# Rows spread over partitions by DMA through DRAM instead of by TensorE, halves swapped by VectorE, biases made three products at a time

## The chip, the cores and the metric

One NeuronCore of a Trainium2 chip runs the whole program in one launch. The metric is device time in microseconds, the median of several runs. Instructions run on TensorE (PE; its weight loads are shown apart, as PEld), VectorE (DVE), ScalarE (ACT) and GpSimd (POOL). DMAs are issued from the queues of SP, ACT and POOL.

## The reference, cut to what matters

Two blocks run on 512 tokens of width 1024, all in float32. The first has two hybrid layers; each holds sparse attention with an index (DSA), stick-breaking attention, and an mLSTM, whose outputs are gated and merged. The second has a feed-forward part, a mixing layer (an S5 state-space scan, dilated attention in three patterns, cross attention to a memory) and another feed-forward part. The change touches four places:

```python
# mLSTM: a weight exp(b_t - b_s + i_s - m_t) for every pair (t, s); m_t is a row over tokens, one per head
w_intra = jnp.exp(log_d - m_row[..., None])
# dilated attention: scores get a bias from rel_table by the bucket of the distance, per pattern and head;
# the three patterns' outputs are summed with shares that are a softmax over the patterns, per token and head
# S5: complex numbers with real and imaginary parts on 64 partitions each; a rotation needs both parts
x_re, x_im = abar_re * x_re - abar_im * x_im, abar_re * x_im + abar_im * x_re
```

## The kernel before, in words

Activations stand feature by feature: 128 features on partitions, 512 tokens along the free axis. Every big product is split in three (`three`, L292 to L294), with high and low parts of both factors in F32R: a weight block comes by DMA on SP's queue as `raw` (L255), ACT casts it to `whi` (L260) and DVE forms `wlo` (L261). A 512-column F32R product is one pass of PE. A product of plain F32, as in the four places below, is two passes with two weight loads (PE rows count passes).

The program is written as one stream of instructions. Its framework (Tile) orders each engine's instructions at build time from the dependencies and from tile slots in rings (`row`, `fr`, PSUM banks `b0` to `b7`), with the order of the text as priority; weight loads are raised by an offset (`woff`). On the chip each engine then keeps that order. So PE's stream mixes stages: a product with few columns stands between products of another stage, and topk rounds on DVE (`dsa_choose`, L606 and L607, needed by `dsa` at the end of a layer) stand wherever DVE had room. In the mixing layer `together` (L1182) interleaves three streams by costs: `mix_products`, `ssm` and `attention`; the last ends with `shares`, whose result `oa` is needed by the first `wup` product (L1157 on).

The four places, in order of time:

- **mLSTM rows** (`ml_gates` L756, `mlstm` L824). A scan on DVE (L814) leaves `M`, 4 partitions (heads) by 512 tokens. For each head a product of a one-hot column of the identity with `M` (L860) puts that head's row on all 128 partitions, in the PSUM bank of `av`; ACT reads it in the exponentials of L866. 2 layers x 4 heads = 8 products.
- **Biases** (`biases` L1365, called between the two halves of the first layer's mLSTM). Per pattern DVE copies the bias table out to 128 columns per head (L1374, L1375); per head one product with one-hot buckets (L1379, 33 rows) gives 128 equal rows, ACT copies them (L1381), a POOL DMA stores them in `bd` (L1382). 12 products. `dilated_qkv` reads `bd` in the mixing layer (L1390).
- **SSM halves** (`ssm` L1719). Rotation into and out of the scan needs the other half's product: `y = sin * p` over 128 partitions (L1751, L1764), a product with a permutation that swaps the halves (L1755, L1766), an add or subtract from PSUM (L1756, L1768). 4 groups x 2 = 8 products.
- **Shares** (`shares` L1475). Per pattern: 4 transposes bring the shares to 4 partitions (L1496, shown under the helper's L490), ACT copies them (L1498), two products with 4 rows spread them over 64 partitions per head (L1501), and DVE multiplies the stored outputs `od` by them (L1505, L1509), reading PSUM. 12 transposes, 6 products.

The constants of the permutation, the spreading and a selection matrix `sel` are part of one tile loaded at the start (L1832); `sel` is copied once to F32R (L1833).

Of the kernel before, what the change touches and what calls it, by code (L numbers as in the profile page):

```python
# [8 lines left out]
F32 = mybir.dt.float32  # L9
# [8 lines left out]
P = 128  # L18
S = 512
D = 1024  # L20
NB = 4
# [66 lines left out]
def constants():  # L88
    parts = []
    at = 0  # L90

    def put(name, a):
        nonlocal at
        a = np.asarray(a, np.float32).reshape(P, -1)
        CONST[name] = (at, a.shape[1])
        at += a.shape[1]
        parts.append(a)

    i = np.arange(P)
# [5 lines left out]
    sel = np.zeros((P, P))  # L105
    for r in range(P):
        if r % 64 < 16:
            sel[r, r % 64] = 1.0
            sel[r, 64 + r % 64] = 1.0
    put("sel", sel)  # L110
# [9 lines left out]
    sp = np.zeros((P, 2, P))  # L120
    for h in range(4):
        sp[h, h // 2, 64 * (h % 2):64 * (h % 2) + 64] = 1.0
    put("spread", sp)
    put("swap", np.roll(np.eye(P), 64, axis=1))
    put("oz", np.tile([1.0, 0.0], (P, 4)))
    return np.concatenate(parts, axis=1)

# [58 lines left out]
def prepare(x):  # L186
    x = {k: np.asarray(v) for k, v in x.items()}
    out = {}
    out["consts"] = constants()
    out["vecs"] = vectors(x)  # L190
    out["xT"] = np.ascontiguousarray(x["x"][0].T.reshape(8, P, S).transpose(1, 0, 2))
    w = x["w_in"]
# [32 lines left out]
class Prog:  # L225
# [530 lines left out]
    def ml_gates(self, l):  # L756
# [58 lines left out]
        self.mlM = M  # L815
# [8 lines left out]
    def mlstm(self, l, W, u):  # L824
# [32 lines left out]
        for e in range(2):  # L857
            h = 2 * u + e
            pm = self.av()
            nc.tensor.matmul(pm, self.c("ident")[0:4, h:h + 1].to_broadcast([4, P]), self.mlM, start=True, stop=True)  # L860
# [504 lines left out]
    def biases(self):  # L1365

        nc, ap = self.nc, self.ap
        rel = self.t(ap, [32, 12], tag="rel")
        nc.gpsimd.dma_start(rel, self.A["rel"])
        oh = self.t(ap, [P, 896], tag="r4", bufs=2)[0:33]  # L1370
        nc.gpsimd.dma_start(oh, self.A["oneh"])
        for p in range(3):
            relb = self.row().rearrange("p (h n) -> p h n", h=4)
            nc.vector.memset(relb[32:33], 1.0)  # L1374
            nc.vector.tensor_copy(relb[0:32], rel[:, 4 * p:4 * p + 4].unsqueeze(2).to_broadcast([32, 4, P]))  # L1375
            w, at, n = self.BANDS[p]
            for h in range(4):
                ps = self.lt()
                nc.tensor.matmul(ps[:, :w], relb[0:33, h, :], oh[:, at:at + w], start=True, stop=True)  # L1379
                r = self.row()  # L1380
                nc.scalar.copy(r[:, :w], ps[:, :w])  # L1381
                nc.gpsimd.dma_start(self.bd[4 * p + h][0:P * w].rearrange("(p w) -> p w", w=w), r[:, :w])  # L1382
# [92 lines left out]
    def shares(self):  # L1475
# [14 lines left out]
        nc.vector.reciprocal(sm, sm)  # L1490
        acc = []
        for p in range(3):
            nc.vector.tensor_mul(sh[:, p, :, 0], sh[:, p, :, 0], sm)
            ps = self.lt()
            for b in range(NB):
                self.tr(ps[0:4, b * P:(b + 1) * P], sh[:, p, b, 0, :])  # L1496
            wt = self.row()
            nc.scalar.copy(wt[0:4, :], ps[0:4, :])  # L1498
            for m in range(2):
                ps = self.lt()  # L1500
                nc.tensor.matmul(ps, self.c("spread")[0:4, m * P:(m + 1) * P], wt[0:4, :], start=True, stop=True)  # L1501
                o = self.fr()
                nc.sync.dma_start(o, self.od[:, 2 * p + m, :])
                if p == 0:
                    nc.vector.tensor_mul(o, o, ps)  # L1505
                    acc.append(o)
                else:
                    t = self.row()
                    nc.vector.tensor_mul(t.rearrange("p (i r) -> p r i", r=4), o.rearrange("p (r i) -> p r i", r=4),  # L1509
                                         ps.rearrange("p (i r) -> p r i", r=4))  # L1510
# [207 lines left out]

    def ssm(self, W, sp):  # L1719
# [11 lines left out]
        for mt in range(4):  # L1731
# [19 lines left out]
            nc.vector.tensor_mul(y, sin, p)  # L1751
            nc.vector.tensor_mul(x, cos, p)
            yield True
            p = self.bank("py")
            nc.tensor.matmul(p, self.c("swap"), y, start=True, stop=True)  # L1755
            nc.vector.tensor_add(x, x, p)  # L1756
# [7 lines left out]
            nc.vector.tensor_mul(y, sin, w)  # L1764
            p = self.bank("py")
            nc.tensor.matmul(p, self.c("swap"), y, start=True, stop=True)  # L1766
            nc.vector.tensor_mul(x, cos, w)
            nc.vector.tensor_sub(x, x, p)  # L1768
# [23 lines left out]
    def run(self):  # L1792
# [14 lines left out]
        self.gd = dp.tile([16, 32, 240], F32, name="gd")  # L1807
        self.kd = dp.tile([P, 4, 256], F32, name="kd")
# [5 lines left out]
        with tc.tile_pool(name="at", bufs=1, reuse_waits="tile") as ap:  # L1814
# [18 lines left out]
            nc.scalar.copy(self.selr, self.c("sel"))  # L1833
# [45 lines left out]
```

## Time and profile before

| | us |
|---|---|
| median of 3 runs | 2619.22 (2613.62 to 2619.58) |
| profiled execution | 2615.3 |
| its span, first to last instruction | 2613.5 |
| PE busy in the span | 2568.2 |
| PE weight loads busy | 2113.5 |
| DVE busy | 1673.0 |
| ACT busy | 1179.3 |
| POOL busy | 265.9 |

A row of the timeline has the start of an instruction in microseconds from the start of the span, its length, engine, line, operation, output and inputs, shape and how many are joined in the row (x2); in brackets the idle time of the engine before it and what ended that. Lengths of products overlap, so what one costs PE is read from the starts of its neighbours.

### The profile page before, as it was taken

Reading aid. Unit: us, or ns where it says so; the run is one execution under the profiler, and the core shown is the slowest. Engines: PE = TensorE matmul, PEld = TensorE weight load, DVE = VectorE, ACT = ScalarE, POOL = GpSimd, SP = SyncE. Lnnn points to the kernel's source line nnn. Section 1 sums busy time; section 2 is a strip of 40 time slices with the busy share of each in tenths; the row PEclk is TensorE's granted clock in tenths of the full one; section 3 lists DMA queues with packets and bytes.
Section 4 is the critical chain, followed back from the end, with each engine's and each line's share of the span. In section 5 each row is a group of like instructions: output and inputs, shape, how many; then the busy total and the mean of one; then the engine's idle time right before and its main releaser. Section 6 shows DMA issues by size and latency. Waiting matters only on the chain.

```text
span 2613.5 us, 36025 instructions
## 1 busy us (share of the span) xinstructions
PE 2568.2 (98%) x13206; PEld 2113.5 (81%) x13206; DVE 1673.0 (64%) x3696; ACT 1179.3 (45%) x2290; POOL 265.9 (10%) x573
## 2 busy tenths in 40 slices
PE   8999999999999999999999999999999999999998
PEld 8888778788888777878888888877876778888798
DVE  8999975654699998665479665374333445555423
ACT  6665656743466565663342332233444233333322
POOL 0010000110000000001002782000000100000000
PEclk9999999999999999999999999999999999999999
DMA  6222232353322223235333334354433444322332
GB/s 191 85 101 85 93 107 97 104 178 125 113 73 90 85 89 114 88 113 178 121 130 106 133 124 150 106 170 144 119 93 115 158 153 151 107 97 97 121 89 81
DMA packets 115105, 305.56 MB, mean 117 GB/s; under 512 B 29210, under 2 KB 36506, under 8 KB 114928
## 3 DMA queue, kind: packets, MB, share of 16 engines
q1 hardware_dynamic: 87760, 236.23, 27.7%
q0 software_dynamic: 18576, 60.17, 6.6%
q10 hardware_dynamic: 8592, 6.87, 0.8%
q8 instruction: 104, 1.70, 0.3%
q14 instruction: 73, 0.60, 0.1%
HBM read 259.41 MB, written 43.79 MB: 116 GB/s over the span
## 4 chain that ended last, share of the span: by engine, by line
PE 75%; DVE 8%; ACT 3%; issue 1%; DMA 1%; SPq 0%; ACTq 0%; DVEq 0%; POOLq 0%
PE b L292 22%; PE b L293 22%; PE b L294 22%; PE b L490 3%; DVE wlo L261 1%; PE b L633 1%; DVE row L745 1%; PE b L684 1%; PE b L1447 1%; DVE row L744 1%; DVE row L747 1%; DVE row L743 1%; DMA row<-xd 0%; DVE keep L607 0%; PE b L1466 0%
## 5 line engine op out<-in xcount | busy, mean ns | idle before, releaser
L261 DVE TENSOR_TENSOR wlo<-raw,whi 128x1024 fp32r<-128x1024 f32 (+1 forms) x398 | 481.4, 1210 | 505.7 <-ACT whi L260 503.6
L260 ACT CAST whi<-raw 128x1024 fp32r<-128x1024 f32 (+1 forms) x398 | 412.9, 1037 | 646.8 <-PE b L293 486.1
L292 PE MATMUL b<-h,whi 128*128 128x512 f32 x1632 | 642.6, 394 | 0.0
L293 PE MATMUL b<-h,whi 128*128 128x512 f32 x1632 | 642.6, 394 | 0.0
L294 PE MATMUL b<-h,wlo 128*128 128x512 f32 x1632 | 641.0, 393 | 0.4 <-DVE wlo L261 0.4
L292 PEld LDWEIGHTS b<-h,whi 128*128 128x128 f32 x1632 | 307.8, 189 | 62.1 <-issue 2.3
L294 PEld LDWEIGHTS b<-h,wlo 128*128 128x128 f32 x1632 | 307.6, 188 | 61.5 <-DVE wlo L261 0.8
L293 PEld LDWEIGHTS b<-h,whi 128*128 128x128 f32 x1632 | 307.6, 188 | 59.6 <-issue 1.3
L292 PE MATMUL b<-hn,whi 128*128 128x512 f32 x320 | 129.9, 406 | 0.3 <-ACT hn L247 0.3
L294 PE MATMUL b<-hn,wlo 128*128 128x512 f32 x320 | 129.0, 403 | 0.0
L293 PE MATMUL b<-hn,whi 128*128 128x512 f32 x320 | 128.4, 401 | 0.1
L293 PE MATMUL b<-wlo,h 128*128 128x256 f32 x384 | 109.5, 285 | 0.0
L294 PE MATMUL b<-whi,h 128*128 128x256 f32 x384 | 109.2, 284 | 0.0
L292 PE MATMUL b<-whi,h 128*128 128x256 f32 x384 | 109.2, 284 | 0.0
L490 PE MATMUL b<-cst,row 128*128 128x128 f32 x452 | 88.9, 288 | 18.8 <-DVE row L747 11.0
L490 PEld LDWEIGHTS b<-cst,row 128*128 128x128 f32 x452 | 53.3, 143 | 63.1 <-issue 17.8
L1025 ACT ACTIVATE row<-row 128x512 f32<-128x512 f32 x44 | 27.8, 632 | 123.2 <-DVE row L1024 99.4
L292 PE MATMUL b<-whi,g 128*128 128x256 f32 x288 | 82.1, 285 | 0.0
L294 PE MATMUL b<-whi,g 128*128 128x256 f32 x288 | 82.1, 285 | 0.0
L293 PE MATMUL b<-wlo,g 128*128 128x256 f32 x288 | 81.9, 284 | 0.0
L292 PE MATMUL b<-yb,whi 128*128 128x512 f32 x192 | 75.9, 396 | 0.0
L294 PE MATMUL b<-yb,wlo 128*128 128x512 f32 x192 | 75.5, 393 | 0.0
(591 smaller groups left out, 5240.7 us busy)
## 6 DMA issues: line engine op xcount, KB each, us to landing
raw<-in_win_dram SPq DMA_DIRECT2D x190, 512.0 KB, 3.7
raw<-in_ffn_in_dram SPq DMA_DIRECT2D x88, 512.0 KB, 3.7
raw<-in_ffn_down_dram SPq DMA_DIRECT2D x40, 512.0 KB, 3.5
raw<-in_wbr_dram SPq DMA_DIRECT2D x24, 512.0 KB, 3.4
mxd<-fr POOLq DMA_DIRECT2D x48, 256.0 KB, 2.6
fr<-mxd POOLq DMA_DIRECT2D x48, 256.0 KB, 3.9
raw<-in_wout_dram SPq DMA_DIRECT2D x24, 512.0 KB, 3.7
yd<-row POOLq DMA_DIRECT2D x24, 256.0 KB, 2.6
```

What stands on the lines that cost most here:

```text
L260: nc.scalar.copy(hi, raw)
L261: nc.vector.tensor_sub(lo, raw, hi.bitcast(F32))
L292: mm(ps, a[0], b[0], start=first, stop=False)
L293: mm(ps, a[0], b[1], start=False, stop=False)
L294: mm(ps, a[1], b[0], start=False, stop=last)
L490: self.nc.tensor.transpose(out, in_, self.c("ident"))
L633: self.nc.tensor.matmul(o[:, c], V(sb), PT[i][:, sb, c], start=sb == 0 and i == 0, stop=sb == 3 and i == 1)
L684: nc.tensor.matmul(p[:, :nn], Q[h][:, tb * P:(tb + 1) * P], kk[i][:, :nn], start=i == 0, stop=i == 1)
L743: nc.vector.scalar_tensor_tensor(e[:, :n], e[:, :n], 1.0, st[:, :n], op0=ALU.min, op1=ALU.mult)
L744: nc.vector.scalar_tensor_tensor(sg[:, :n], sg[:, :n], 0.0, e[:, :n], op0=ALU.max, op1=ALU.add)
L745: nc.vector.tensor_tensor_scan(e[:, :n][:, ::-1], st[:, :n][:, ::-1], self.one.to_broadcast([P, n]), 1.0, op0=ALU.mult, op1=ALU.min)
L1025: nc.scalar.activation(th, t, AF.Tanh, scale=0.5)
```

## The change

- mLSTM: `M` is stored to a DRAM tile `md` after the scan, and each head's row is loaded from it with a broadcast over 128 partitions into an SBUF tile `pm`, both on POOL's queue. The tile shares a slot with `R` for odd heads.
- Biases: one product per pattern with the table's 4 columns as weights gives 4 rows; ACT copies them, POOL stores them in `br`, and four POOL DMAs per pattern copy a row, broadcast, from `br` to `bd`.
- Shares: all 12 columns are transposed together, 4 transposes in all; one copy, one store to `wd`, and 12 loads (64 partitions each), all on ACT's queue; DVE multiplies from SBUF.
- SSM: `crossed` makes the product with two DVE instructions of 64 partitions, each writing the other half; no swap product.
- `sel` is an input of its own, loaded into a `row` slot; three matrices leave the constants.

```diff
-        self.mlM = M
+        nc.gpsimd.dma_start(self.md, M)
...
-            pm = self.av()
-            nc.tensor.matmul(pm, self.c("ident")[0:4, h:h + 1].to_broadcast([4, P]), self.mlM, start=True, stop=True)
+            pm = self.t(self.hp if e else ap, [P, S], tag="R" if e else "pm", bufs=1)
+            nc.gpsimd.dma_start(pm, self.md[h:h + 1, :].to_broadcast([P, S]))
...
         for p in range(3):
-            relb = self.row().rearrange("p (h n) -> p h n", h=4)
-            nc.vector.memset(relb[32:33], 1.0)
-            nc.vector.tensor_copy(relb[0:32], rel[:, 4 * p:4 * p + 4].unsqueeze(2).to_broadcast([32, 4, P]))
             w, at, n = self.BANDS[p]
-            for h in range(4):
-                ps = self.lt()
-                nc.tensor.matmul(ps[:, :w], relb[0:33, h, :], oh[:, at:at + w], start=True, stop=True)
-                r = self.row()
-                nc.scalar.copy(r[:, :w], ps[:, :w])
-                nc.gpsimd.dma_start(self.bd[4 * p + h][0:P * w].rearrange("(p w) -> p w", w=w), r[:, :w])
+            ps = self.lt()
+            nc.tensor.matmul(ps[0:4, :w], rel[:, 4 * p:4 * p + 4], oh[:, at:at + w], start=True, stop=True)
+            r = self.row()
+            nc.scalar.copy(r[0:4, :w], ps[0:4, :w])
+            nc.gpsimd.dma_start(self.br[4 * p:4 * p + 4, :w], r[0:4, :w])
+            for h in range(4 * p, 4 * p + 4):
+                nc.gpsimd.dma_start(self.bd[h][0:P * w].rearrange("(p w) -> p w", w=w), self.br[h:h + 1, :w].to_broadcast([P, w]))
...
+        wt = self.t(ap, [P, NB, 3, 4], tag="wt")
+        for p in range(3):
+            nc.vector.tensor_mul(wt[:, :, p], sh[:, p, :, 0], sm)
+        ps = self.lt()
+        for b in range(NB):
+            self.tr(ps[0:12, b * P:(b + 1) * P], wt[:, b].rearrange("p x h -> p (x h)"))
+        wr = self.row()
+        nc.scalar.copy(wr[0:12, :], ps[0:12, :])
+        nc.scalar.dma_start(self.wd, wr[0:12, :])
...
-                ps = self.lt()
-                nc.tensor.matmul(ps, self.c("spread")[0:4, m * P:(m + 1) * P], wt[0:4, :], start=True, stop=True)
-                o = self.fr()
+                o, t = self.fr(), self.row()
                 nc.sync.dma_start(o, self.od[:, 2 * p + m, :])
+                for e in range(2):
+                    h = 4 * p + 2 * m + e
+                    nc.scalar.dma_start(t[64 * e:64 * e + 64, :], self.wd[h:h + 1, :].to_broadcast([64, S]))
...
+    def crossed(self, out, a, b):
+        for i in range(2):
+            r, q = slice(64 * i, 64 * i + 64), slice(64 - 64 * i, 128 - 64 * i)
+            self.nc.vector.tensor_mul(out[q, :], a[r, :], b[r, :])
...
-            nc.vector.tensor_mul(y, sin, p)
+            self.crossed(y, sin, p)
             nc.vector.tensor_mul(x, cos, p)
...
-            nc.tensor.matmul(p, self.c("swap"), y, start=True, stop=True)
-            nc.vector.tensor_add(x, x, p)
+            nc.vector.tensor_add(x, x, y)
...
-            nc.scalar.copy(self.selr, self.c("sel"))
+            sel = self.row()[:, :P]
+            nc.sync.dma_start(sel, self.A["sel"])
+            nc.scalar.copy(self.selr, sel)
```

## Rows read from the trace of the kernel before

**Rows 1.** The page, busy microseconds by engine, share of the span, instructions.

```profile
PE 2568.2 (98%) x13206; PEld 2113.5 (81%) x13206; DVE 1673.0 (64%) x3696; ACT 1179.3 (45%) x2290; POOL 265.9 (10%) x573
```

**Rows 2.** Timeline of PE around the first head's row of the mLSTM.

```profile
108.08 0.28 PE L294 MATMUL b<-whi,h 128*128 128x256 f32 x1
108.29 1.12 PE L860 MATMUL b<-mlM,cst 4*128 4x512 f32 x2
...
109.68 0.40 PE L293 MATMUL b<-q,q 128*128 128x512 f32 x1
109.91 0.40 PE L294 MATMUL b<-q,q 128*128 128x512 f32 x1
```

**Rows 3.** Windows: busy us (instructions) by engine, PE's granted clock, DMA share, GB/s.

```profile
200.00:300.00 100.00, 95.45 (x522) 78.18 (x522) 98.53 (x218) 59.51 (x118) 2.72 (x5) 1.00 0.25 84
...
1760.00:1940.00 180.00, 179.90 (x951) 142.38 (x950) 77.52 (x210) 72.06 (x167) 0.00 (x0) 1.00 0.41 121
...
139.00:143.00 4.00, 4.00 (x11) 3.15 (x12) 3.09 (x9) 3.35 (x11) 1.12 (x3) 0.57 0.38 139
2039.00:2044.00 5.00, 5.00 (x12) 2.97 (x12) 4.91 (x7) 0.62 (x1) 0.00 (x0) 0.66 0.36 105
```

**Rows 4.** Tile mlM: durations in ns min/median/max, first and last start us, forms.

```profile
L860 PEld LDWEIGHTS b<-mlM,cst x16: 180/183/241, 108.3 to 811.7; 4*128 4x128 f32 x16
...
L814 DVE TENSOR_TENSOR_SCAN mlM<-cst,mlin,b x8: 458/460/468, 83.8 to 762.8; 4x128 f32<-4x128 f32 x8
```

**Rows 5.** The page, DMA issues: count, KB each, median us from issue to landing.

```profile
mxd<-fr POOLq DMA_DIRECT2D x48, 256.0 KB, 2.6
fr<-mxd POOLq DMA_DIRECT2D x48, 256.0 KB, 3.9
```

**Rows 6.** Timeline of PE at the biases.

```profile
136.14 2.84 PE L1379 MATMUL b<-r,row 33*128 33x384 f32 x8
...
139.62 0.63 PE L294 MATMUL b<-h,wlo 128*128 128x512 f32 x1
...
142.60 0.46 PE L292 MATMUL b<-h,whi 128*128 128x512 f32 x1
...
144.81 1.99 PE L1379 MATMUL b<-r,row 33*128 33x256 f32 x8
```

**Rows 7.** Timeline of PE at a swap product.

```profile
1772.49 0.40 PE L294 MATMUL b<-hn,wlo 128*128 128x512 f32 x1
1772.74 1.10 PE L1755 MATMUL b<-srow,cst 128*128 128x512 f32 x2
...
1773.90 0.39 PE L293 MATMUL b<-hn,whi 128*128 128x512 f32 x1
```

**Rows 8.** Line L1751, the product that is to be halved: durations in ns.

```profile
L1751 DVE TENSOR_TENSOR srow<-sv,b x4: 686/688/689, 1771.3 to 1915.4; 128x512 f32<-128x512 f32 x4
```

**Rows 9.** Lines by form, 2015 to 2040: transposes of the shares; busy us, mean ns, idle.

```profile
L490 PE MATMUL b<-cst,sh 128*4 128x128 f32 x12 | 1.8, 272 | 0.0
```

**Rows 10.** Timeline of PE at the spreading products of the shares.

```profile
2022.29 0.39 PE L292 MATMUL b<-xk,whi 128*128 128x512 f32 x1
2022.61 1.98 PE L1501 MATMUL b<-row,cst 4*128 4x512 f32 x4
...
2024.86 0.40 PE L294 MATMUL b<-xk,wlo 128*128 128x512 f32 x1
...
2038.83 2.06 PE L1501 MATMUL b<-row,cst 4*128 4x512 f32 x4 [0.89 <-DVE row L1509]
...
2043.97 0.39 PE L292 MATMUL b<-hn,whi 128*128 128x512 f32 x1
...
2047.45 0.39 PE L292 MATMUL b<-xk,whi 128*128 128x512 f32 x1
```

**Rows 11.** Timeline of DVE where the last part of oa is made.

```profile
2046.00 0.69 DVE L248 TENSOR_TENSOR xk<-fr,xk 128x512 fp32r<-128x512 f32 x1 [1.63 <-ACT xk L247]
```

More of the change, by code (lines that the diff above doesn't have):

```diff
@@ L104, in constants @@
     put("tri", (i[:, None] <= i[None, :]) * 1.0)
[L105 to L110, printed above, removed]
     pos = np.arange(S, dtype=np.float32)
@@ L119, in constants, with selects @@
     put("csgn", sgn)
-    sp = np.zeros((P, 2, P))
-    for h in range(4):
-        sp[h, h // 2, 64 * (h % 2):64 * (h % 2) + 64] = 1.0
-    put("spread", sp)
-    put("swap", np.roll(np.eye(P), 64, axis=1))
     put("oz", np.tile([1.0, 0.0], (P, 4)))
     return np.concatenate(parts, axis=1)
+def selects():
+    sel = np.zeros((P, P), np.float32)
+    for r in range(P):
+        if r % 64 < 16:
+            sel[r, r % 64] = 1.0
+            sel[r, 64 + r % 64] = 1.0
+    return sel
 def onehots():
@@ L189, in prepare @@
     out["consts"] = constants()
+    out["sel"] = selects()
     out["vecs"] = vectors(x)
@@ L1367, in biases @@
         nc, ap = self.nc, self.ap
-        rel = self.t(ap, [32, 12], tag="rel")
-        nc.gpsimd.dma_start(rel, self.A["rel"])
+        rel = self.t(ap, [33, 12], tag="rel")
+        nc.vector.memset(rel[32:33], 1.0)
+        nc.gpsimd.dma_start(rel[0:32], self.A["rel"])
         oh = self.t(ap, [P, 896], tag="r4", bufs=2)[0:33]
@@ L1372, in biases @@
         for p in range(3):
-            relb = self.row().rearrange("p (h n) -> p h n", h=4)
-            nc.vector.memset(relb[32:33], 1.0)
-            nc.vector.tensor_copy(relb[0:32], rel[:, 4 * p:4 * p + 4].unsqueeze(2).to_broadcast([32, 4, P]))
             w, at, n = self.BANDS[p]
-            for h in range(4):
-                ps = self.lt()
-                nc.tensor.matmul(ps[:, :w], relb[0:33, h, :], oh[:, at:at + w], start=True, stop=True)
-                r = self.row()
-                nc.scalar.copy(r[:, :w], ps[:, :w])
-                nc.gpsimd.dma_start(self.bd[4 * p + h][0:P * w].rearrange("(p w) -> p w", w=w), r[:, :w])
+            ps = self.lt()
[5 more added lines that the diff above has]
+                nc.gpsimd.dma_start(self.bd[h][0:P * w].rearrange("(p w) -> p w", w=w), self.br[h:h + 1, :w].to_broadcast([P, w]))
     def dilated_qkv(self, W, p):
@@ L1490, in shares @@
         nc.vector.reciprocal(sm, sm)
+        wt = self.t(ap, [P, NB, 3, 4], tag="wt")
[7 more added lines that the diff above has]
+        nc.scalar.dma_start(self.wd, wr[0:12, :])
         acc = []
         for p in range(3):
-            nc.vector.tensor_mul(sh[:, p, :, 0], sh[:, p, :, 0], sm)
-            ps = self.lt()
[L1495 to L1498, printed above, removed]
             for m in range(2):
-                ps = self.lt()
-                nc.tensor.matmul(ps, self.c("spread")[0:4, m * P:(m + 1) * P], wt[0:4, :], start=True, stop=True)
-                o = self.fr()
+                o, t = self.fr(), self.row()
                 nc.sync.dma_start(o, self.od[:, 2 * p + m, :])
+                for e in range(2):
+                    h = 4 * p + 2 * m + e
+                    nc.scalar.dma_start(t[64 * e:64 * e + 64, :], self.wd[h:h + 1, :].to_broadcast([64, S]))
                 if p == 0:
-                    nc.vector.tensor_mul(o, o, ps)
+                    nc.vector.tensor_mul(o, o, t)
                     acc.append(o)
                 else:
-                    t = self.row()
-                    nc.vector.tensor_mul(t.rearrange("p (i r) -> p r i", r=4), o.rearrange("p (r i) -> p r i", r=4),
-                                         ps.rearrange("p (i r) -> p r i", r=4))
+                    tv = t.rearrange("p (i r) -> p r i", r=4)
+                    nc.vector.tensor_mul(tv, o.rearrange("p (r i) -> p r i", r=4), tv)
                     nc.vector.tensor_add(acc[m], acc[m], t)
@@ L1750, in ssm @@
             x, y = srow(), srow()
-            nc.vector.tensor_mul(y, sin, p)
+            self.crossed(y, sin, p)
             nc.vector.tensor_mul(x, cos, p)
             yield True
-            p = self.bank("py")
-            nc.tensor.matmul(p, self.c("swap"), y, start=True, stop=True)
-            nc.vector.tensor_add(x, x, p)
+            nc.vector.tensor_add(x, x, y)
             w = srow()
@@ L1763, in ssm @@
             x, y = srow(), srow()
-            nc.vector.tensor_mul(y, sin, w)
-            p = self.bank("py")
-            nc.tensor.matmul(p, self.c("swap"), y, start=True, stop=True)
+            self.crossed(y, sin, w)
             nc.vector.tensor_mul(x, cos, w)
-            nc.vector.tensor_sub(x, x, p)
+            nc.vector.tensor_sub(x, x, y)
             yield True
@@ L1807, in run @@
         self.gd = dp.tile([16, 32, 240], F32, name="gd")
+        self.md = dp.tile([4, S], F32, name="md")
+        self.wd = dp.tile([12, S], F32, name="wd")
+        self.br = dp.tile([12, 384], F32, name="br")
         self.kd = dp.tile([P, 4, 256], F32, name="kd")
```

## The prediction

> **What bounds the kernel now.** I read four views: the page for the shares of the engines, the windows for stages, the timeline of PE for what one product costs, and tiles and DMA issues for how far ahead each input is. PE is busy for 2568.2 of 2613.5 us [rows 1]; that alone proves little, since lengths overlap. The timeline decides: 512-column products start every 0.23 us with no gap (109.68 to 109.91), and what stands between two of them moves all that follow [rows 2]. So a product taken out of PE's stream is worth the distance by which it held its neighbours apart, if the next work is ready. Whether it is depends on the stage. In the mixing layer DVE is busy 77.5 of 180 us and PE 179.9: clearly PE. In the stick-breaking stretch DVE has 98.5 of 100 us and PE still 95.5: two full engines, though DVE's time there holds topk rounds that can wait [rows 3].
>
> **mLSTM rows: minus 10.0 us.** The product (two passes) stands after a 256-column product that starts at 108.08; the second product behind it starts at 109.68 [rows 2]. Without it that distance is 0.12 + 0.23, so it costs 1.60 - 0.35 = 1.25 us. The tile has 16 weight loads, so 8 products: 10.0 us [rows 4]. In their place stand two stores of `M` and 8 loads on POOL's queue. The trace has no broadcast load; the nearest row is a 256 KB load by POOL, 3.9 us to landing, behind a 256 KB store, 2.6 us [rows 5]: 6.5 us for the first head, 3.9 for the others. Bounds per head are nothing (hidden) and those figures (exposed). I take nothing: the scan starts at 83.8, the first product at 108.3 [rows 2, 4], so the row lands some 17 us early, and with slots `pm` and `R` in place of the one PSUM bank the next head's load can start while the last is read. If the cover goes, the exponentials of L866 are late, and behind them on ACT the weight casts. ACT reads the same 128x128 pieces as before; I count no change there.
>
> **Biases: minus 6.5 us.** Four products of a pattern take 2.84 us at 384 columns and 1.99 at 256; the third pattern is like the second, 6.8 in all [rows 6]. One product per pattern remains with the same moving columns, a quarter: 1.7, so 5.1 saved. Further, right after the first group the products start 0.43 us apart: from 139.62 to 142.60 there are 7 distances, 2.98 us where 7 x 0.23 = 1.61 belong [rows 6]. The granted clock of that stretch is 0.57, so PE was part of the time at 1.2 GHz instead of 2.4 [rows 3]. What PE did before is four products on 33 of 128 rows, with no idle time. With one such product in their place I expect the slow stretch to go: 1.4 us. Lower bound nothing: it may come at another place. POOL gets 3 stores and 12 copies where it had 12 stores; each group of copies waits for a store to land, 3 x 2.6 = 7.8 us in which the next POOL work stands behind [rows 5]. That work is the load of head 2's row, which lies a whole set of q, k and v products later, so I count nothing; `bd` is read in the mixing layer, hundreds of microseconds on. DVE loses three copies and ACT nine, both hidden now.
>
> **SSM halves: minus 7.6 us.** Neighbours of a swap product start at 1772.49 and 1773.90, 1.41 instead of 0.46: 0.95 us, eight times, 7.6 us [rows 7]. DVE pays: each 128-partition product of 0.69 us becomes two of 64 [rows 8]. Bounds: half (the work is halved) or the full 0.69 each (the length follows the 512 elements of a partition). I take the full: 8 x 0.69 = 5.5 us more on DVE, hidden, since DVE has over 100 us of idle time in this stage [rows 3]. The dependent chain loses a trip through PE.
>
> **Shares: minus 9.8 us, plus 3.** Twelve transposes take 1.8 us; four remain, 1.2 saved [rows 9]. The spreading products come as three pairs, the second like the first. First pair: 2022.29 to 2024.86, 2.57 instead of 0.46, so 2.1 us; twice 4.2. Third pair: a wait of 0.89 for DVE, then 2038.83 to 2043.97 with 7 products, 5.14 instead of 1.61, so 3.5; 4.4 with the wait, 8.6 in all [rows 10]. About 1.5 of that is again a clock of 0.66 in this stretch [rows 3]. What is late next: the first `wup` product starts at 2047.45 [rows 10] and the last piece of `oa` is done at 2046.00 + 0.69, 0.8 us earlier [rows 11]. The chain on DVE that makes `oa` does not get shorter by the 4.4 us that PE gains after 2031, so PE may wait 4.4 - 0.8 = 3.6 us. On top comes a trip through DRAM, 6.5 us by the nearest rows [rows 5], and ACT's queue now holds a store and 12 loads, with the casts of weights behind them. The trip starts some 20 us before `oa` is due, when the first copy ends (before 2022.61), so it is covered. Bounds: nothing (the build-time order puts a gate product first) and 3.6 + 6.5 = 10.1. I take 3, near the rows of the chain.
>
> `sel` and the constants: one small DMA more on SP at the start; its copy is needed first by `dsa`, hundreds of microseconds later; nothing.
>
> **Sum.** 10.0 + 6.5 + 7.6 + 9.8 = 33.9 off, 3 on: 30.9 less. The profiled execution took 2615.3 (span 2613.5 and 1.8 around it), so 2584.4. The median of the runs is 3.9 above that execution: 2619.2 - 30.9 = 2588.
>
> **A page against it.** The rows above price a removed product by its neighbours' starts, 1.25 us [rows 2]. The Trainium skill (Trainium Kernel Development and Optimization, Performance Expectations) says that matmul busy time is a poor measure, because matmuls are pipelined, and that weight-load time is a better one. Read so, PE has slack (2113.5 of 2613.5 us, 81% [rows 1]) and a removed pass is worth its load only.
>
> **Rivals.**
> - *Only the weight loads count.* 16 + 18 + 16 + 12 = 62 passes go, at 0.18 us each [rows 4]: 11.2 us, 2619.2 - 11.2 = 2608. Against it: starts without gaps [rows 2]. Chance 0.08.
> - *DVE takes over.* If DVE sets the pace of the first layers, where it is at 98.5% next to the mLSTM [rows 3], the 16.5 us of rows and biases come back as waits for it; add the 10.1 at `oa` and 5.5 for the halves: 33.9 - 32.1 = 1.8, so 2617, no change. For it: PE is at 95.5 there. Against it: topk rounds fill DVE and may move later. A reshuffled order that eats the gain would look the same. Chance 0.13.
> - *Head rows come late, slower than before.* POOL's queue is in order. If each load is issued only when its exponentials are due, 8 x 3.9 and two stores of 2.6 are exposed, 36.4 us [rows 5], and each such wait brings a slow-clock stretch like the one after the 0.89 wait, 8 x 1.4: 47.6 on, 33.9 off, 2619.2 + 13.7 = 2633. It decides once a load is issued less than 3.9 us ahead at nearly all heads. For it: stores of finished heads stand in the same queue. Against it: POOL's 10% [rows 1] and 24 us of lead [rows 2, 4]. Chance 0.06.
>
> **How the numbers follow.** The forecast has 0.73. Its own range: down to 2613.6 (fastest run) - 33.9 = 2580, and 3 less if a slow-clock stretch or a wait more goes, 2577; up, with the 10.1 at `oa` and both clock gains lost (2.9), 2619.2 - 20.9 = 2598. To hold 8 in 10 with the first rival the range goes to 2608. A measurement can tell about 0.3%, 8 us, from no change: faster is the forecast and the first rival, 0.81; same 0.13; slower 0.06.
>
> **What would show it.** Right: no L860 on PE, mLSTM loads landing over 10 us before L866; 3 products in the biases and a clock of 1.0 at 139 to 143 and around the shares; no waits of PE for POOL's or ACT's DMAs; PE's idle time about as now; DVE some 3 to 6 us busier in the mixing layer. Wrong: PE waits over 1 us for exponentials' outcomes or for `oa`, DVE near 100% further on, or starts of big products that lie as far apart as before where nothing stands between them.

## The result and the profile after

The kernel after takes 2586.0 us (median of 4 runs, 2583.7 to 2589.1); the kernel before took 2618.9 on the same chip (4 runs, 2613.6 to 2619.6). The ratio is 0.9884, 95% interval 0.9871 to 0.9897: faster by 1.2%. The forecast of 2588 is 2 us off, well inside its range. The profiled execution has a span of 2583.6 us where before had 2613.5, 29.9 less; the sum of the prediction was 30.9. The sections below show that the total came nearer than its parts, and that some 5 us of the 29.9 are peculiar to the one trace of before.

The page of after, in the columns of [rows 1]:

```profile
PE 2538.2 (98%) x13136; PEld 2100.6 (81%) x13136; DVE 1674.0 (65%) x3699; ACT 1176.7 (46%) x2279; POOL 271.5 (11%) x586
```

PE has 70 passes fewer and 30.0 us less busy time, as much as the span lost. Its idle time is the same: the gaps between its instructions sum to 37.4 us after and 37.5 before. PE still sets the end.

Where the 29.9 us went is read by the start of one and the same instruction in both traces:

| landmark | before | after | gained in the stage | forecast |
|---|---|---|---|---|
| first index product of layer 0 (L589) | 70.3 | 74.2 | +3.9 | 0 |
| a product ahead of layer 0's first row (L294) | 104.1 | 106.3 | -1.7 | 0 |
| first product of layer 0's `dsa` (L684) | 419.4 | 410.3 | -11.3 | -11.5 (4 rows, biases) |
| first product of layer 1's `dsa` | 1062.8 | 1046.9 | -6.8 | -5.0 (4 rows) |
| last product of the SSM (L1773) | 1950.9 | 1927.3 | -7.7 | -7.6 |
| an output product behind the shares (L293) | 2123.7 | 2096.9 | -3.2 | -6.8 |
| a product in the second feed-forward (L294) | 2444.0 | 2418.0 | +0.8 | 0 |
| one near its end (L294) | 2485.6 | 2455.5 | -4.1 | 0 |
| end of the span | 2613.5 | 2583.6 | +0.2 | 0 |

The second landmark stands at the same place of PE's order in both kernels. The first does not: in after, eight more passes stand ahead of it, 8 x 0.23 = 1.8 us, so 1.7 of its 3.9 us come back at once. What is left of the start, 2.2 us, is scatter: over all versions the product at 104.1 comes between 0.4 us earlier and 2.7 us later, whatever was changed. Two stages of the prediction came true almost to the tenth (SSM, layer 0), one within 2 us (layer 1), one gave half (shares), and at the start and at the end, where nothing was forecast, the time moved by 2.2 and 4.1 us in opposite directions.

The windows of after, columns as in [rows 3]; the third is the mixing layer, moved by the 16 to 17 us gained up to there:

```profile
139.00:143.00 4.00, 4.00 (x18) 2.79 (x18) 3.86 (x17) 3.58 (x15) 2.99 (x6) 1.00 0.17 58
200.00:300.00 100.00, 97.00 (x499) 78.25 (x498) 98.49 (x209) 59.82 (x119) 2.19 (x4) 1.00 0.27 92
1743.00:1923.00 180.00, 179.86 (x972) 145.26 (x970) 85.66 (x223) 74.53 (x177) 0.00 (x0) 1.00 0.43 128
2018.00:2025.00 7.00, 6.45 (x16) 5.11 (x17) 4.68 (x6) 3.16 (x5) 1.09 (x2) 0.53 0.33 115
```

The clock at the biases is 1.00 where it was 0.57; below it turns out that this is not the change's doing. DVE has 8.1 us more in the mixing layer and PE is as full as before. The last row is new: behind the shares PE runs at 0.53, that is at its lower level of 1.2 GHz nearly throughout. What happened there, first on PE, then on ACT, then on DVE of the same kernel:

```profile
2013.73 0.40 PE L294 MATMUL b<-hn,wlo 128*128 128x512 f32 x1
2018.55 0.79 PE L292 MATMUL b<-hn,whi 128*128 128x512 f32 x1 [4.42 <-ACT fr L1121]
2019.14 0.63 PE L293 MATMUL b<-hn,whi 128*128 128x512 f32 x1
2019.56 0.63 PE L294 MATMUL b<-hn,wlo 128*128 128x512 f32 x1
...
2024.64 0.39 PE L292 MATMUL b<-hn,whi 128*128 128x512 f32 x1
2024.86 0.40 PE L293 MATMUL b<-hn,whi 128*128 128x512 f32 x1
```

```profile
2008.35 1.05 ACT L260 CAST whi<-raw 128x1024 fp32r<-128x1024 f32 x1 [4.95 <-DMA row<-wd]
2008.43 7.03 ACTq L1508 DMA_DIRECT2D row<-wd  x4
2017.90 0.60 ACT L1121 ACTIVATE fr<-b 128x512 f32<-128x512 f32 x1 [8.50 <-DVE row L1514]
```

```profile
2011.52 1.08 DVE L1514 TENSOR_TENSOR row<-fr,row 128x512 f32<-128x512 f32 x1 [4.23 <-DMA fr<-od]
...
2016.74 1.07 DVE L1514 TENSOR_TENSOR row<-fr,row 128x512 f32<-128x512 f32 x1
```

PE waits 4.42 us for a gate's tanh (L1121), which writes an `fr` tile and empties a PSUM bank. The tanh waited 8.50 us, and what ended that is the shares' product L1514. That product reads a stored output `o`, which is also an `fr` tile. The ring has four; two hold the running sums (`acc`), and each `o` keeps one from its load until its row has come from DRAM. Before, the tanh (L1120) waited for PE (9.1 us in all) and once, 0.2 us, for DVE, never for a slot. Behind its wait, PE's products in after start 0.43 us apart until 2024.3, where 0.23 is usual.

### The profile page after: what moved, and what is told of

The parts are those of the page before. It is cut to its first block, busy times and chain, and to the rows that moved or that the text cites. A ratio compares the mean times of both kernels' runs of the same rounds, so it can differ in the third digit from the quotient of the medians.

```text
span 2583.6 us, 35854 instructions
## 1 busy us (share of the span) xinstructions
PE 2538.2 (98%) x13136; PEld 2100.6 (81%) x13136; DVE 1674.0 (65%) x3699; ACT 1176.7 (46%) x2279; POOL 271.5 (11%) x586
## 4 chain that ended last, share of the span: by engine, by line
PE 48%; issue 12%; DVE 4%; DMA 1%; ACT 1%; POOL 0%; SPq 0%; POOLq 0%; ACTq 0%; DVEq 0%
PE b L292 15%; PE b L293 15%; PE b L294 15%; PE b L490 1%; PE b L633 1%; DVE row L745 1%; DVE wlo L261 1%; PE b L684 0%; DVE row L744 0%; DVE row L747 0%; DVE row L743 0%; DMA fr<-od 0%; DVE keep L607 0%; PE b L1695 0%; DVE m L606 0%
## 5 line engine op out<-in xcount | busy, mean ns | idle before, releaser
L293 PE MATMUL b<-h,whi 128*128 128x512 f32 x1632 | 641.8, 393 | 0.0
L294 PE MATMUL b<-h,wlo 128*128 128x512 f32 x1632 | 640.4, 392 | 0.0
L294 PEld LDWEIGHTS b<-h,wlo 128*128 128x128 f32 x1632 | 307.1, 188 | 60.7 <-issue 0.9
L293 PEld LDWEIGHTS b<-h,whi 128*128 128x128 f32 x1632 | 307.2, 188 | 59.9 <-issue 1.4
L293 PE MATMUL b<-hn,whi 128*128 128x512 f32 x320 | 128.9, 403 | 0.1
L294 PE MATMUL b<-hn,wlo 128*128 128x512 f32 x320 | 128.4, 401 | 0.0
L293 PE MATMUL b<-wlo,h 128*128 128x256 f32 x384 | 109.3, 285 | 0.0
L294 PE MATMUL b<-whi,h 128*128 128x256 f32 x384 | 109.2, 284 | 0.0
L294 PE MATMUL b<-whi,g 128*128 128x256 f32 x288 | 81.9, 284 | 0.0
L293 PE MATMUL b<-wlo,g 128*128 128x256 f32 x288 | 81.6, 283 | 0.0
L292 PEld LDWEIGHTS b<-hn,whi 128*128 128x128 f32 x320 | 61.0, 190 | 20.6 <-ACT fr L1121 4.8
L625 DVE TENSOR_TENSOR pt<-b,pt 128x128 fp32r<-128x128 f32 (+3 forms) x128 | 61.5, 485 | 22.2 <-ACT pt L624 21.4
```

Source lines behind the costliest of these rows:

```text
L292: mm(ps, a[0], b[0], start=first, stop=False)
L293: mm(ps, a[0], b[1], start=False, stop=False)
L294: mm(ps, a[1], b[0], start=False, stop=last)
L625: nc.vector.tensor_sub(PT[1][:, 0:tb + 1, c], pv, PT[0][:, 0:tb + 1, c].bitcast(F32))
```

## Experiments

Each version is compared by the landmarks above; its time stands beside the median of the kernel before on the same chip (2614.1, 2614.5 or 2617.1 us, 7 runs each). A version without a ratio was run once. Differences from the trace of before, in us:

| version | L589 | 104.1 | `dsa` 0 | `dsa` 1 | SSM last | 2123.7 | 2444.0 | end |
|---|---|---|---|---|---|---|---|---|
| after | +3.9 | +2.2 | -9.1 | -15.9 | -23.6 | -26.8 | -26.0 | -29.9 |
| SSM part alone | +1.7 | +1.7 | +0.7 | +0.8 | -7.4 | -6.9 | -6.4 | -9.7 |
| biases alone | +0.1 | +0.1 | -9.1 | -9.2 | -9.3 | -8.7 | -8.2 | -11.8 |
| shares alone | +0.7 | +0.7 | -0.2 | -0.1 | -0.1 | -3.6 | -2.0 | -5.6 |
| after without the rows | +2.1 | +0.4 | -7.3 | -7.3 | -15.3 | -17.0 | -16.0 | -20.3 |
| before, rows twice | +0.8 | +0.8 | +7.6 | +14.9 | +15.5 | +14.6 | +14.7 | +11.0 |
| before, full biases | +2.5 | +2.7 | -0.8 | -0.8 | -0.5 | +3.4 | +3.6 | +0.2 |

### The SSM part alone

The kernel before with this edit of the change and no other (the same at the second place, L1764 to L1768):

```diff
-            nc.vector.tensor_mul(y, sin, p)
+            self.crossed(y, sin, p)
...
-            nc.tensor.matmul(p, self.c("swap"), y, start=True, stop=True)
-            nc.vector.tensor_add(x, x, p)
+            nc.vector.tensor_add(x, x, y)
```

> The kernel before with the SSM part alone (two DVE halves, no swap products). Theory (neighbours' distance is the price): from the first to the last SSM product the time shrinks by 8 x 0.95 = 7.6 us, total about 2611. Rival (only weight loads count): 16 loads x 0.19 = 3 us, 2616. Rival (DVE pays): 0 or longer, 2619 or more, and DVE's share in the stretch near 1.

Measured: 2605.5 us (before 2614.1). The SSM stage is 7.7 us shorter (its first product +0.3, its last -7.4), as in after. DVE's halves, from the lines of after:

```profile
L1727 DVE TENSOR_TENSOR srow<-sv,b x8: 680/685/690, 1755.4 to 1900.8; 64x512 f32<-64x512 f32 x8
L1727 DVE TENSOR_TENSOR srow<-sv,srow x8: 684/685/687, 1761.4 to 1907.5; 64x512 f32<-64x512 f32 x8
```

A product on 64 partitions takes as long as one on 128 ([rows 8]: 688 ns), so the upper bound was right: 16 x 0.685 in place of 8 x 0.69 is 5.5 us more on DVE, and none of it shows in the end of the stage. The term stands; the price by weight loads, 3 us, does not.

### The biases alone

The kernel before with the new `biases`, three products in all in place of twelve, and no other edit:

```diff
-                nc.tensor.matmul(ps[:, :w], relb[0:33, h, :], oh[:, at:at + w], start=True, stop=True)
+            nc.tensor.matmul(ps[0:4, :w], rel[:, 4 * p:4 * p + 4], oh[:, at:at + w], start=True, stop=True)
...
+                nc.gpsimd.dma_start(self.bd[h][0:P * w].rearrange("(p w) -> p w", w=w), self.br[h:h + 1, :w].to_broadcast([P, w]))
```

> The kernel before with the new biases alone (three products, br and bd through DRAM). Theory (neighbours' distance and the clock): 5.1 + 1.4 = 6.5 us less by the end of the first layer. Rival (only weight loads count): 18 x 0.18 = 3.3. Rival (DVE sets the pace): under 2, since DVE loses only three copies of 0.9 us.

Measured: 2603.5 us (before 2614.5). Up to layer 0's stick-breaking the gain is 6.9 us (its first product L735 goes from 211.1 to 204.2), and it is 9.1 at the first `dsa` product: 2.2 more come inside the stick-breaking stretch. Versions that leave this layer as it was (SSM alone, shares alone) also make up 0.9 to 1.0 us in it, all of it at the biases, where the trace of before has its slow stretch and theirs have none (next section). So some 8 of the 9.1 are the biases', 6 of them ahead of the stick-breaking. The waits of PE between 200 and 420 us (engine, line waited for, total us, times, longest), before and then in this version:

```profile
PE b L490 <- DVE row L747: 5.5, 16, 0.7
PE b L490 <- DVE hv L915: 1.1, 1, 1.1
PE b L735 <- DVE pt L625: 0.7, 3, 0.3
```

```profile
PE b L490 <- DVE row L747: 3.9, 12, 0.5
PE b L490 <- ACT whi L260: 1.1, 3, 0.5
PE b L490 <- ACT fr L955: 0.3, 1, 0.3
```

The waits for DVE fall from 7.3 to 3.9 us, those for ACT rise to 1.4: 2.0 less. DVE is full there [rows 3], so a table copy taken from it a little earlier may be worth something, where the prediction had it hidden. That these copies are what the 2.2 us come from is not shown, and one run speaks against a fixed price: after without the rows (below) has the same biases and gains 0.2 us in that stretch.

### The biases on 128 rows

Is it the 33 rows that bring the slow stretch at 139.6? The kernel before, with 95 rows of zeros added to both factors of the bias products:

```diff
-            nc.vector.memset(relb[32:33], 1.0)
+            nc.vector.memset(relb, 0.0)
+            nc.vector.memset(relb[32:33], 1.0)
...
-                nc.tensor.matmul(ps[:, :w], relb[0:33, h, :], oh[:, at:at + w], start=True, stop=True)
+                nc.tensor.matmul(ps[:, :w], relb[:, h, :], oh[:, at:at + w], start=True, stop=True)
```

> The kernel before with the twelve bias products on all 128 rows (zeros in 95 of them, two more kinds of memset on DVE) instead of 33; the results are the same. Theory (products on few rows let the clock fall although PE is not idle): no stretch at the lower clock at the biases, 1.4 us less there. Rival (the clock fell there by the time of many small F32 products, whatever their rows): the slow stretch stays and the time is that of the kernel before.

Measured: 2615.5 us (before 2614.5), span 0.2 longer. Windows of this version at the biases, and at the shares, where the program is that of before:

```profile
140.00:144.00 4.00, 4.00 (x16) 2.73 (x15) 3.95 (x15) 3.08 (x12) 0.93 (x2) 1.00 0.33 103
...
2041.00:2049.00 8.00, 7.36 (x16) 4.62 (x17) 6.11 (x8) 0.97 (x2) 0.55 (x1) 0.63 0.21 70
```

The same number of products with the same columns, on all rows: the clock stays at 1.00 at the biases, as in after. That alone seems to say that the 33 rows were the cause. But the SSM part alone and the shares alone hold the twelve products as before has them, on 33 rows. The first group in the timeline of the SSM part alone, then the same window in that version and in the shares alone:

```profile
137.87 2.84 PE L1379 MATMUL b<-r,row 33*128 33x384 f32 x8
```

```profile
139.00:143.00 4.00, 4.00 (x16) 2.67 (x15) 3.33 (x11) 3.61 (x11) 1.62 (x3) 1.00 0.40 148
139.00:143.00 4.00, 4.00 (x18) 2.88 (x17) 3.17 (x10) 3.89 (x12) 1.31 (x4) 1.00 0.40 148
```

The clock is 1.00 there too, and so it is in the version with the rows' products doubled. So the padding shows nothing: the same products bring the slow stretch in one trace and not in three others, and what brings it is open. Its price is the 1.0 us that the SSM part alone and the shares alone make up at this place. This version makes up 3.5 us in layer 0; padding also moved the bias products in PE's order, and the rest of the 3.5 was not taken apart. Later it loses 3.9 us from the SSM's end to the output product, with slow stretches there that before lacks or has shorter (a clock of 0.67 from 1970 to 1974, and 0.63 from 2041 to 2049).

### The rows' products issued twice

What is one product of L860 worth? The kernel before, each issued a second time:

```diff
             nc.tensor.matmul(pm, self.c("ident")[0:4, h:h + 1].to_broadcast([4, P]), self.mlM, start=True, stop=True)
+            nc.tensor.matmul(pm, self.c("ident")[0:4, h:h + 1].to_broadcast([4, P]), self.mlM, start=True, stop=True)
```

> The kernel before with each of the eight spreading products of the mLSTM issued twice (the second writes the same values). Theory (neighbours' distance): a product costs 1.05 to 1.25 us, so 8.4 to 10 us longer, about 2628. Rival (only weight loads count): 16 x 0.18 = 2.9 us, 2622. Rival (DVE sets the pace in these layers): 0, 2619.

Measured: 2626.3 us (before 2614.1); by layer 1's `dsa` it is 14.1 us more than at the product at 104.1, where 8.4 to 10 were expected. Timeline of PE at the first head and windows behind the second (the added line is 861):

```profile
109.11 1.12 PE L860 MATMUL b<-mlM,cst 4*128 4x512 f32 x2
110.07 1.02 PE L861 MATMUL b<-mlM,cst 4*128 4x512 f32 x2
111.01 0.50 PE L292 MATMUL b<-q,q 128*128 128x512 f32 x1
```

```profile
116.50:120.50 4.00, 4.00 (x16) 3.06 (x15) 2.20 (x10) 2.34 (x9) 0.00 (x0) 0.64 0.01 2
168.00:172.00 4.00, 4.00 (x16) 3.44 (x14) 4.00 (x9) 3.37 (x12) 0.00 (x0) 0.60 0.30 117
779.00:783.00 4.00, 4.00 (x16) 3.08 (x16) 2.63 (x11) 2.48 (x10) 0.00 (x0) 0.60 0.00 0
```

The second product holds its neighbours 0.94 us apart more (110.07 to 111.01), eight of them some 8 us, an estimate from this one. Priced by its weight loads alone, 2 x 0.18, they would cost 3. The other 6 to 7 us go with six new stretches at 1.2 GHz, three of which stand above, with PE busy all the time: one behind the second, the third and the fourth head of each layer. Behind the single products the clock is 1.00 in the trace of before, and no other version has a slow stretch in the layers.

### After without the rows

The eight products put back into the kernel after; everything else as after:

```diff
-            pm = self.t(self.hp if e else ap, [P, S], tag="R" if e else "pm", bufs=1)
-            nc.gpsimd.dma_start(pm, self.md[h:h + 1, :].to_broadcast([P, S]))
+            pm = self.av()
+            nc.tensor.matmul(pm, self.c("ident")[0:4, h:h + 1].to_broadcast([4, P]), self.mlM, start=True, stop=True)
```

> The changed kernel with the eight mLSTM products put back in place of the loads. By the price of the neighbours' distance (1.25 us a product): 5 us more in each layer, 10 in all, some 2596. Theory (in layer 0 DVE is full and hides what PE gains, since biases alone gave all of the 9 us that rows and biases gave together; in layer 1 the rows gave 7): 0 to 2 us more at the first stick-breaking product that matters to dsa in layer 0, 5 to 8 more in layer 1, 2592 to 2595. By the weight loads alone (0.18 a pass, 16 passes): 3 us more, 2589.

Measured: 2595.0 us, 9.0 more than the median of after (before on this chip 2617.1). Taken from the product at 104.1 on, layer 0 is 7.7 us shorter than before where after is 11.3 shorter, and layer 1 is the same as before where after is 6.8 shorter: the rows give 3.6 and 6.8, together 10.4. The price by the neighbours' distance (10) holds in sum. The theory that layer 0 hides it all does not: from one landmark to the next it hides 1.4 of 5. Why layer 1 gives 1.8 more than its four products is open.

That DRAM does not hold the rows up is seen in after. POOL's and ACT's timelines at the first head, then all loads on the page of DMA issues, columns as in [rows 5]:

```profile
96.30 0.52 POOL L815 DMA_DIRECT2D md<-mlM  x1 [22.47 <-DVE mlM L814]
98.98 0.59 POOL L861 DMA_DIRECT2D pm<-md  x1 [2.15 <-DMA md<-mlM]
```

```profile
102.62 1.87 ACT L867 ACTIVATE row<-pm,mlG 128x128 f32<-128x128 f32 x6 [0.21 <-DMA pm<-md]
```

```profile
row<-wd ACTq DMA_DIRECT2D x12, 128.0 KB, 3.7
...
pm<-md POOLq DMA_DIRECT2D x4, 256.0 KB, 3.6
R<-md POOLq DMA_DIRECT2D x4, 256.0 KB, 3.8
```

The one wait in eight loads is the first, 0.21 us. The first load of layer 1 lands at 760.06, and ACT reads it at 760.08.

### The shares alone

The kernel before with the new `shares` and no other edit:

```diff
-                nc.tensor.matmul(ps, self.c("spread")[0:4, m * P:(m + 1) * P], wt[0:4, :], start=True, stop=True)
...
+                    nc.scalar.dma_start(t[64 * e:64 * e + 64, :], self.wd[h:h + 1, :].to_broadcast([64, S]))
```

> The kernel before with the new shares alone. The prediction's term was 9.8 us off and 3 on, 6.8 less. Theory (the shares hold the fr slots that a gate's tanh wants, PE waits some 4 us for it and then runs some 7 us at half clock): 2 to 4 us less at the last fr load of the output stage (L1133), so 2610 to 2612 at the end, or 2608 if the unexplained 3 us at the end of the second feed-forward come too; a wait of PE of 3 to 5 us for ACT's fr of L1121 and a granted clock near 0.5 for some 7 us behind it. Rival (the shares cost only what was predicted and the loss comes from the other parts' order): 6 to 10 us less, no such wait, 2604 to 2608.

Measured: 2609.7 us (before 2617.1), 3.5 us less from the SSM's end to the output product where 6.8 were forecast, and the same wait without any of the other parts. Timeline of PE, and the window behind it:

```profile
2038.88 0.40 PE L294 MATMUL b<-hn,wlo 128*128 128x512 f32 x1
2042.82 0.79 PE L292 MATMUL b<-hn,whi 128*128 128x512 f32 x1 [3.54 <-ACT fr L1120]
```

```profile
2042.00:2049.00 7.00, 6.18 (x20) 4.97 (x21) 4.92 (x7) 3.27 (x5) 1.10 (x2) 0.76 0.31 105
```

The wait belongs to this edit. The clock behind it was at the lower level for about half of the 7 us, less than in after.

The 3.5 have to be read beside a place that the change does not touch. Some 20 us behind the SSM, PE waits 1.3 us for ACT (L1455 in before) in every version. Behind this one wait the clock fell in seven of the fourteen traces and stayed at 1.00 in the other seven. Here, where it fell, and in before, in the same window:

```profile
1968.00:1975.00 7.00, 5.47 (x18) 3.50 (x17) 3.33 (x6) 4.90 (x11) 0.00 (x0) 0.76 0.49 131
```

```profile
1968.00:1975.00 7.00, 5.47 (x25) 3.32 (x25) 4.28 (x10) 5.87 (x13) 0.54 (x1) 1.00 0.46 131
```

Where it falls, PE's products behind it are 1.5 us later. After has no such stretch either, so the shares alone gave 5.0 where after got 3.2.

### The shares' loads on another queue

First suspicion: the 12 loads stand on ACT's queue ahead of the tanh. The kernel after with them on POOL's, then on SP's queue:

```diff
-                    nc.scalar.dma_start(t[64 * e:64 * e + 64, :], self.wd[h:h + 1, :].to_broadcast([64, S]))
+                    nc.gpsimd.dma_start(t[64 * e:64 * e + 64, :], self.wd[h:h + 1, :].to_broadcast([64, S]))
```

> The changed kernel with the twelve loads of the shares' rows issued from POOL's queue instead of ACT's; nothing else. Theory (ACT's queue is blocked): in the changed kernel the gate's tanh stood 8.5 us behind loads that waited for row slots, so PE waited 4.4 us and then had 6.8 us at the lower clock, some 2.9 us lost; here that wait and the slow stretch go, about 7 us less than the changed kernel: 2579. Rival (the chain on DVE that makes oa, with its fr slots, sets the time): PE waits as long for oa instead, 2583 to 2587.

> The same with the twelve loads on SP's queue. Theory (ACT's queue is blocked): as from POOL, about 2579, unless weight loads on SP now stand behind the loads that wait for row slots, in which case PE waits for a weight cast a few us and it comes to 2581 to 2586. Rival (chain for oa): 2583 to 2587 with a wait for xk.

Measured: POOL 2586.9 us, ratio 0.9894 (0.9878 to 0.9911); SP 2584.4, ratio 0.9885 (0.9870 to 0.9900). Neither differs from after in its time. Timeline of PE with POOL:

```profile
2020.66 0.79 PE L292 MATMUL b<-hn,whi 128*128 128x512 f32 x1 [7.17 <-ACT fr L1121]
```

On SP that wait is 4.59 us. From the SSM's end to the output product, with the 1.5 us of the stretch behind L1455 taken out (both have it, after has not), POOL gains 1.4 us and SP 3.3, where after gains 3.2. It is not ACT's queue. The Trainium skill (DMA: Bandwidth & Descriptors, Issuing engines are not separate DMA queues) says that DMAs of all issuing engines share the same DMA engines, so that spreading them saves only time of issuing; the times of these two runs agree with it.

### A fifth slot, and slots of another ring

If the slot is what is missed, one more must help. The kernel after, in `mix`:

```diff
         self.rowbufs = 4
+        self.frbufs = 5
```

> The changed kernel with five fr slots instead of four in the mixing layer. Theory (fr slots): one more slot lets one tanh go ahead, so at least half of the wait of 4.4 us goes, and with it perhaps the slow clock: 2579 to 2584. Rival (row slots or the DRAM trip): no change, 2586, with the wait in the same place.

Measured: 2580.0 us (2577.9 to 2582.5), ratio 0.9865 (0.9843 to 0.9888). PE at the shares, and the windows there:

```profile
2014.66 0.50 PE L292 MATMUL b<-hn,whi 128*128 128x512 f32 x1 [1.22 <-ACT fr L1121]
...
2017.68 0.72 PE L292 MATMUL b<-xk,whi 128*128 128x512 f32 x2 [1.12 <-ACT xk L247]
...
2021.05 0.50 PE L293 MATMUL b<-xk,whi 128*128 128x512 f32 x1 [1.01 <-DVE xk L248]
```

```profile
2010.00:2017.00 7.00, 5.34 (x22) 3.68 (x20) 5.74 (x7) 1.53 (x2) 0.00 (x0) 1.00 0.68 198
2017.00:2024.00 7.00, 5.31 (x21) 3.90 (x22) 5.51 (x8) 2.18 (x4) 1.10 (x2) 1.00 0.44 152
```

The one long wait is three short ones and the clock stays at 1.00. The output product behind the shares starts at 2092.3, where after has 2096.9; 2.3 of these 4.6 us were there by the SSM's end. The last two waits are for `xk`, the parts of `oa`: the chain that the prediction had named now comes to light behind the slot. In the next version `o` takes the SSM's `srow` slots, with four `fr` as in after:

```diff
-                o, t = self.fr(), self.row()
+                o, t = self.srow(), self.row()
```

> The changed kernel with the stored dilated outputs of the shares loaded into the SSM's row slots (six, free by then) instead of the four fr slots, which the gates' tanh outputs share. Theory now (fr slots): the gate's tanh waits for an fr slot that the shares hold, its PSUM bank stays full and PE waits; with slots of their own the wait of 4.4 us and the slow clock behind it (2.9 us) go: 2579. Rival (the row slots or the trip through DRAM set the time of oa): the wait turns up at the first wup product instead, 2583 to 2587.

Measured: 2582.2 us, ratio 0.9874 (0.9855 to 0.9893). The wait for the tanh is gone and one for `xk` is there, in PE's timeline:

```profile
2019.75 1.22 PE L292 MATMUL b<-xk,whi 128*128 128x512 f32 x2 [2.66 <-ACT xk L247]
```

Its clock from 2018 to 2025 is 0.58, so it gains little on after at this place. Last, both together, with the loads on ACT's queue and then on SP's:

> The changed kernel with a fifth fr slot in the mixing layer and the shares' stored outputs loaded into the state-space part's free srow slots. Theory (both waits of PE at the shares, for the tanh's fr slot and for xk, are waits for slots): all waits over 1 us at the shares go and no half-clock stretch stands there, 2575 to 2579. Rival (with slots enough the chain load, DVE product, xk is what is late, as with the own slots alone): a wait of 1 to 3 us for xk stays, 2579 to 2583, no better than the fifth slot alone (2580).

> The same with the twelve loads of the shares' rows on SP's queue instead of ACT's. Theory (ACT's queue costs about half a microsecond of ACT for each load, and the tanh stands behind them): what is left of the wait goes, 2574 to 2578, 1 to 3 us below the version with the loads on ACT. Rival (the queue does not matter, as it did not without the slots; on SP the loads stand between weight loads): the same within 2 us, or 1 to 2 us more.

Measured: 2580.4 us, ratio 0.9859 (0.9844 to 0.9874), and 2579.0, ratio 0.9857 (0.9841 to 0.9873). In both a wait for `xk` stays (2.66 and 2.15 us): the rivals hold. With slots enough, the chain of the load, the product on DVE and `xk` is what is late, and neither the queue nor more slots take its wait away; which link of it is the late one was not tested. Three versions lie at 2579 to 2580; the best median is that with SP, 7 us under after. The intervals of all these ratios overlap with after's, so that they beat it rests on the timelines as well. Gained from the SSM's end to the output product, in us:

| version | gained | of it lost behind L1455 | gained without that |
|---|---|---|---|
| after | 3.2 | 0 | 3.2 |
| fifth slot | 5.4 | 1.5 | 6.9 |
| `srow` slots | 2.2 | 1.5 | 3.7 |
| both | 6.3 | 0 | 6.3 |
| both, loads on SP | 8.5 | 0 | 8.5 |

## Why the prediction was right, point by point

**What bounds the kernel.** Right. PE's busy time fell by as much as the span, its idle time stayed, and a removed or added product was worth its neighbours' distance: 10.4 for the rows where 10.0 stood, 0.94 for a doubled product. The rival that only weight loads count falls with that; its 11.2 us are a third of what was gained.

**Rows.** The size is right in sum, the cover was not. The row did not land some 17 us early. The prediction took the first scan's start, 83.8 [rows 4], but the store has to wait for the last of the four, which ends at 89.9 in before; in after it ends at 96.0, and ACT asks for the row at 102.4, where the product in before started at 108.3. The load landed 0.2 us after ACT was ready. The price of nothing held with a margin of nothing at the first head of each layer; at the other six the row lands 3.9 to 39 us ahead, because the slots are free. The sign named for it, over 10 us, fails at four of the eight heads. The rival of late rows fell, by less than it seemed.

**Biases.** Some 8 us alone where 6.5 stood, and 6.7 beside the rows (11.3 in layer 0, less 3.6 and less the 1.0 of the slow stretch). PE at the biases in after:

```profile
137.77 1.24 PE L1377 MATMUL b<-r,rel 33*4 33x384 f32 x4
138.94 0.50 PE L293 MATMUL b<-h,whi 128*128 128x512 f32 x1
139.37 0.59 PE L1377 MATMUL b<-r,rel 33*4 33x256 f32 x2
139.89 0.50 PE L294 MATMUL b<-h,wlo 128*128 128x512 f32 x1
```

The first two products hold 1.17 us, the third 0.52: 1.7, as worked out, and the clock is at its upper level. So 5.1 us for the products was near: 6 came ahead of the stick-breaking. The step that failed is the clock. The prediction gave the slow stretch to the four products on 33 rows and counted 1.4 us for its going; three versions with the same products have no such stretch, and in two of them its absence is worth 1.0 us. Its size was nearly met by chance: the trace of before had the stretch. The 2.2 us more inside the stick-breaking, where PE waits for DVE, stand in no term; the prediction had DVE's copies hidden.

**DVE takes over.** Fell as a rival: DVE is at 98.49 of 100 us from 200 to 300, as before, yet the gains of both layers reach the end. A part of it is true of layer 0, where the rows give 3.6 of 5.0.

**SSM.** Right in both terms, 7.7 for 7.6, with DVE's upper bound. DVE is 8.1 us busier in the mixing layer's window, more than the 3 to 6 that were named, and it cost nothing there.

**Shares.** The term was 9.8 off and 3 on; 3.2 came, and 5.0 with the shares alone. The gross gain and the bounds for the wait (0 to 10.1) were right, the step "what is late next" was not: it named `oa`, the data, and the first thing late was a slot, in which the shares' operands now wait for DRAM. The wait of 4.4 us is near the taken 3, but it brought 0.47 x 7 = 3.3 us of lower clock with it, which the prediction had counted as a gain here. 9.8 - 4.4 - 3.3 is 2.1, within about 1 of the 3.2. The sign that was named for it, no clock below 1.0 around the shares, failed.

**What was in no step.** The 2.2 us of the start are scatter, and 1.7 more at the first index product are order, as said above; which edit changed that order was not tested. At the end of the second feed-forward PE waits less for loads of `row<-xd` (waits of PE from 2400 us on, before, then after):

```profile
PE b L490 <- DMA row<-xd: 3.8, 3, 1.9
```

```profile
PE b L490 <- DMA row<-xd: 1.1, 3, 0.5
```

With it goes a stretch at a clock of 0.66 (2480 to 2485 before; 1.00 at 2455 to 2460 after): 4.1 us. Every version in the table above gains 3.3 to 4.4 us there, the one with doubled products and the one with full biases too. So it is no effect of a part of this change, but of the one trace of before, and why is open. Without the 2.2 of the start, the 4.1 of the end and the 1.0 of before's slow stretch at the biases the sum is 27.0, not 29.9. Against 30.9 that is 3.6 too little at the shares, 1.2 too little in layer 0 without that stretch, 1.8 too much in layer 1, and 1.0 lost behind the shares. So the total came out near the forecast partly by luck.

## What to carry to other kernels

When an operand that PE made in PSUM is fetched by DMA instead, ask which ring holds its partner while the fetch is under way, and who else writes to that ring: here two of four slots were sums, and the fetch kept a gate, a PSUM bank and PE waiting. Price a small F32 product between F32R products by the distance of its neighbours, not by weight loads, and look at the granted clock behind it. Compare versions by the same instruction at several landmarks that stand at the same place of the engine's order: strays of 2 and 4 us with opposite signs do not show in a total. And before a slow-clock stretch is put down to what stands ahead of it, look for the same instructions in a second trace: here the stretch at the biases, and the one behind L1455, were in some traces and not in others.

## What the runs showed of the hardware

- The granted clock fell to its lower level with PE busy throughout, six times where each product on 4 rows was issued twice (0.60 to 0.64). After four F32 products on 33 rows it fell in the trace of before (0.57) and stayed at 1.00 in three others with the same products.
- Behind one and the same wait of 1.3 us (L1455) it fell in seven of fourteen traces. At the shares it fell around waits of 7.17, 4.59, 4.42, 3.54 and 2.66 us, and stayed at 1.00 around one of 2.15 and three of 1.0 to 1.2. The Trainium skill (TensorE: Matmul & The Clock Gate, HAM oscillation) tells of clocks lost to waits for DMA. The falls around the long waits are like that, though what PE waits for here is ACT, and ACT for a product or a slot behind a load; the falls with PE busy are another case.
- DVE takes 685 ns for 512 elements on 64 partitions and 688 on 128.
- In the lines of after, loading 4 columns of F32 weights takes PE 78 to 83 ns a pass and 128 columns took 183 [rows 4]: shorter, but far from a thirty-second.
- The twelve loads of one row each to 64 partitions land 2.7 to 8.2 us after their issue, the eight to 128 partitions after 3.4 to 5.1.
